# A hybrid gMLP and pooling layer on one core: edge rows loaded behind the first row tile, their norm chain placed behind the first copies, and their turned form given a tile of its own

## The chip, the core and the metric

The kernel runs on one core of one Trainium2 chip. The metric is the device time of one execution in microseconds (us). The inputs are full size: one prompt stream of 4096 frames with 1024 channels, and one sample stream of 32 frames.

## What is computed

One layer of a streaming encoder, once for the prompt and once for the sample rows:

```python
h = rmsnorm(x, norm_g)
u, v, z_a, xb, z_b = split(h @ w_in)                      # w_in: 1024 x 5120
v_n = layernorm(v, ln_v_g, ln_v_b)
a = u * chunk_mlp(v_n, w_spatial, b_spatial) * silu(z_a)  # 128x128 mixing matrix per head
x_ext = concatenate([pool_past, xb])                      # 15 earlier rows, then the new ones
b = pool_mix(x_ext, pos0, w_pool, pool_scale) * silu(z_b) # trailing means of 2/4/8/16 rows, then w_pool
y = rmsnorm(x + concatenate([a, b]) @ w_out, final_g)
```

Further outputs are the last 15 rows of `x_ext` of both streams (the pooling state) and the sample's `v_n`.

## The kernel before

**The work as a whole.** Nearly all the time goes into large matrix products in float32 accuracy. Each operand is split into a rounded part and a rest (L109 casts on ScalarE, L82 subtracts on VectorE), and a product of 2x2 blocks is made with seven block products instead of eight. Those matmuls stand at L184 and, for the output projection, at L703 to L705. The span before them, some 57 us, prepares what they need, and the change lies wholly there.

**The opening phase** has four strands, written in one loop over eight row tiles `i` (`for i in range(KT)`), whose parts a scheduler then puts in order on each engine. Some instructions are wrapped in `tc.keep_in_program_order`, which fixes their place among the others that are wrapped; the rest may be moved.

- *Combined weights.* The part of `w_in` that makes `xb` is multiplied by `w_pool`. `load_rows(i)` (L247) loads 128 rows of `w_in`, a row tile. `comb_rows(i)` turns it with eight transposes on PE (L418) into two PSUM tiles `tr` and copies each into a buffer `h` (L422; on VectorE for row tiles 0 and 1, on ScalarE from 2 on). `comb_times(i)` multiplies these by the pooling weights (L272, loaded into `op` at L261), ScalarE copies the sums out of PSUM (L436), and GpSimd stores them (L438). For row tile 0 the two halves are called apart: the first half, then row 1's transposes and whatever stands in `before[0]`, then the second half.
- *Edge rows.* The 32 sample rows and the last 16 prompt rows, 48 in all (`edge`, tile `et`), loaded at L264 and L265, with `norm_g` as rows at L266. `edge_stack` makes their RMS norm: a Square with a running sum on ScalarE (L337), one step (L338) and the eleven steps of `rsqrt` (L87 to L92) on VectorE, a scaling on ScalarE (L339). Then PE turns `norm_g` (L341) and the rows (L345), and VectorE writes the result, scaled, into a buffer `h` (L346). `State.times` multiplies it by pairs of row tiles (L192, for the pooling state), and a store to `stk` (L559) keeps it for the sample's later work.
- *v weights.* Four loads of two tiles (L283, L284), each split into seven pairs of operands in `slot` (L109, L82, with sums at L105). `PACE` says how many of these steps follow each row tile.
- *First token tiles.* Pairs of prompt tiles `xt` (L459), normed (Square at L305, scaling at L320 on VectorE) and turned (L466). The first product of the large kind follows at L184, with an operand whose rest is made by VectorE (L82, into `op`).

At the very start PE runs 14 transposes of the identity (`WARM`, L257), which compute nothing that is used.

**Buffers.** `h` tiles rotate over 8 buffers (`h_p`). One of them holds the turned edge rows from L346 until the store to `stk` has landed. Transposes use three PSUM tiles, sums five.

**Queues.** All loads of this phase are issued by SyncE, in the order of the program; the stores of combined weights are issued by GpSimd.

## Time and profile before

| | |
|---|---|
| median of 3 runs (lowest, highest) | 2330.75 us (2328.94, 2331.07) |
| the profiled execution, its span | 2328.7 us, 2326.9 us |
| PE busy, DVE busy, ACT busy | 99%, 76%, 38% of the span |
| granted TensorE clock, mean | 0.998 |
| PE's longest wait | 6.3 us, ended at 11.97 us |

The profile is of one execution. A row of its order of time has the start from the span's beginning, the length, the engine, the line of the kernel, the operation with the tiles it writes and reads, and in brackets how long the engine had been idle and what ended that. PE is TensorE, PEld its weight loads, DVE VectorE, ACT ScalarE, POOL GpSimd, SP SyncE; a small q marks the sequencer of an engine. A float32 matmul has two records, so four matmuls read as x8.

### The profile page before, as it was taken

The numbers are of one execution on the slowest core, as the hardware profiler recorded it, in microseconds if no ns is written. First come the engines' busy times: TensorE is split into PE (matmuls) and PEld (weight loads), VectorE is DVE, ScalarE is ACT, GpSimd is POOL, SyncE is SP. The second block draws the span as 40 slices with busy tenths as digits, with TensorE's granted clock in tenths as the row PEclk, the third lists the DMA queues.
The fourth block names the chain that finished last, engine by engine and source line by source line (L and its number), as shares of the span: only waits on it lengthen the run. The fifth ranks groups of instructions, "written<-read, shape, count | busy, mean of one in ns | idle before, by whom it ended". The sixth has DMA issues, their size and how long they took to land.

```text
span 2326.9 us, 30064 instructions
## 1 busy us (share of the span) xinstructions
PE 2310.8 (99%) x10723; PEld 1892.7 (81%) x10723; DVE 1763.3 (76%) x3172; ACT 893.9 (38%) x1560; POOL 224.9 (10%) x357
## 2 busy tenths in 40 slices
PE   8999999999999999999999999999999999999998
PEld 6888888878878888778888888888888878887887
DVE  6987777867787866887757977778876666588887
ACT  6554544334334333343434433434322222233343
POOL 1000001000121102221000210001200000000000
PEclk9999999999999999999999999999999999999999
DMA  8877777445549454657544483634595555846552
GB/s 281 324 274 281 288 243 247 147 147 181 175 136 352 144 176 133 211 201 254 180 145 158 127 311 120 201 109 154 184 351 169 177 187 183 334 164 205 177 168 91
DMA packets 318221, 470.62 MB, mean 202 GB/s; under 512 B 26068, under 2 KB 225244, under 8 KB 316280
## 3 DMA queue, kind: packets, MB, share of 16 engines
q1 hardware_dynamic: 266872, 379.64, 47.9%
q0 software_dynamic: 21936, 74.14, 8.7%
q10 hardware_dynamic: 29264, 14.94, 2.2%
q8 instruction: 84, 1.38, 0.2%
q14 instruction: 65, 0.53, 0.1%
HBM read 299.19 MB, written 169.47 MB: 201 GB/s over the span
## 4 chain that ended last, share of the span: by engine, by line
PE 95%; DVE 2%; DMA 2%; ACT 0%; issue 0%; SPq 0%; POOL 0%; DVEq 0%; ACTq 0%
PE acc L184 62%; PE acc L703 9%; PE acc L704 9%; PE acc L705 9%; PE sp L956 2%; PE acc L272 1%; PE tr L466 1%; PE acc L192 1%; DMA raw<-in_w_in_dram 1%; DVE wop L82 0%; PE more L192 0%; DMA xt<-in_x_prompt_dram 0%; DVE sum L105 0%; PE tr L418 0%; DMA v_smp<-raw 0%
## 5 line engine op out<-in xcount | busy, mean ns | idle before, releaser
L184 PE MATMUL acc<-slot,wop 128*128 128x512 f32 x5376 | 1240.7, 391 | 1.2 <-DVE wop L82 0.4
L184 PEld LDWEIGHTS acc<-slot,wop 128*128 128x128 f32 x5376 | 1003.3, 188 | 226.1 <-DVE t L156 10.3
L82 DVE TENSOR_TENSOR wop<-raw,wop 128x512 fp32r<-128x512 f32 x520 | 354.5, 686 | 49.7 <-ACT wop L109 43.8
L109 ACT CAST wop<-raw 128x512 fp32r<-128x512 f32 x360 | 221.4, 622 | 337.2 <-PE acc L184 256.5
L703 PE MATMUL acc<-slot,wop 128*128 128x512 f32 x892 | 347.9, 390 | 0.0
L705 PE MATMUL acc<-slot,wop 128*128 128x512 f32 x892 | 347.1, 389 | 0.0
L704 PE MATMUL acc<-slot,wop 128*128 128x512 f32 x892 | 347.0, 389 | 0.0
L184 PE MATMUL acc<-slot,op 128*128 128x512 f32 x1344 | 322.7, 395 | 0.0
L184 PEld LDWEIGHTS acc<-slot,op 128*128 128x128 f32 x1344 | 247.9, 188 | 51.0 <-DVE op L82 0.4
L156 DVE TENSOR_TENSOR t<-acc,t 128x512 f32<-128x512 f32 x256 | 175.7, 686 | 139.7 <-ACT t L165 102.5
L715 DVE TENSOR_TENSOR y<-acc,y 128x512 f32<-128x512 f32 x243 | 164.6, 688 | 133.5 <-PE acc L705 132.4
L703 PEld LDWEIGHTS acc<-slot,wop 128*128 128x128 f32 x892 | 167.4, 188 | 41.4 <-ACT wop L666 6.7
L666 ACT CAST wop<-raw 128x512 fp32r<-128x512 f32 x160 | 99.6, 622 | 252.6 <-PE acc L705 231.0
L705 PEld LDWEIGHTS acc<-slot,wop 128*128 128x128 f32 x892 | 167.4, 188 | 34.9
L704 PEld LDWEIGHTS acc<-slot,wop 128*128 128x128 f32 x892 | 167.4, 188 | 34.5
L82 DVE TENSOR_TENSOR wop<-sum,wop 128x512 fp32r<-128x512 f32 x208 | 142.4, 686 | 61.8 <-ACT wop L109 60.9
L964 POOL DMA_DIRECT2D abT<-t x128 | 69.3, 542 | 799.2 <-DVE t L974 547.0
L109 ACT CAST wop<-sum 128x512 fp32r<-128x512 f32 x144 | 89.2, 622 | 149.2 <-PE acc L184 98.7
L985 DVE TENSOR_TENSOR t<-t 128x527 f32<-128x527 f32 (+3 forms) x160 | 111.3, 696 | 0.4
L165 ACT COPY t<-acc 128x512 f32<-128x512 f32 x64 | 37.5, 585 | 125.6 <-PE acc L184 125.6
L666 ACT CAST wop<-sum 128x512 fp32r<-128x512 f32 x64 | 39.8, 622 | 105.4 <-PE acc L705 72.8
L958 DVE SCALAR_TENSOR_TENSOR t<-sp,lvg,bias 128x512 f32<-128x512 f32 x64 | 47.7, 746 | 41.8 <-PE sp L956 41.7
(210 smaller groups left out, 1872.2 us busy)
## 6 DMA issues: line engine op xcount, KB each, us to landing
raw<-in_w_in_dram SPq DMA_DIRECT2D x126, 512.0 KB, 5.1
xops<-op SPq DMA_DIRECT2D x100, 512.0 KB, 6.3
slot<-xops SPq DMA_DIRECT2D x44, 1024.0 KB, 9.3
abT<-t POOLq DMA_DIRECT2D x128, 256.0 KB, 3.0
raw<-abT SPq DMA_DIRECT2D x64, 512.0 KB, 4.5
wops<-wop SPq DMA_DIRECT2D x56, 512.0 KB, 3.8
slot<-wops SPq DMA_DIRECT2D x14, 2048.0 KB, 9.4
raw<-comb SPq DMA_DIRECT2D x38, 512.0 KB, 4.6
```

The lines of the kernel that those rows point to most:

```text
L82: return nc.vector.tensor_tensor(out, src, hi.bitcast(F32), ALU.subtract)
L109: pair = nc.scalar.copy(hi, src), lo_part(lo, src, hi)
L156: add = lambda o, x, y: nc.vector.tensor_tensor(o, x, y, ALU.add)
L184: mm(acc, stationary(s, k), moving(m, k), start=fresh and n == 0, stop=n == len(terms) - 1, skip_group_check=True)
L666: nc.scalar.copy(t[:, 0], src)
L703: mm(acc, x[:, 0, k, :], w[:, k, 0, c], start=fresh and k == 0, stop=False, skip_group_check=True)
L704: mm(acc, x[:, 0, k, :], w[:, k, 1, c], start=False, stop=False, skip_group_check=True)
L705: mm(acc, x[:, 1, k, :], w[:, k, 0, c], start=False, stop=k == 3, skip_group_check=True)
L715: nc.vector.tensor_tensor(y, self.acc[bank], y, ALU.add)
L958: nc.vector.scalar_tensor_tensor(t1[:, :HALF].rearrange("p (a c) -> p a c", c=P), sp, lg, bias[:, h:h + 1, :].broadcast_to([P, 4, P]), ALU ...
L964: nc.gpsimd.dma_start(abT[row, :, t0:t0 + HALF], t[:, :HALF])
L985: tt(nxt[:, lo:HALO + m], s[:, lo:HALO + m], s[:, lo - step:HALO + m - step], ALU.add)
```

## The change

There are five edits, all in the opening phase.

1. The three loads of the edge rows and of `norm_g` are issued right behind the two halves of row tile 0, ahead of the first two pooling weights; they stood behind these.
2. A Square of one column of the identity is put on ScalarE ahead of all else. It computes nothing that is used; the load of the activation table now belongs to it.
3. `edge_stack` is cut in two. `edge_norm` has the norm; its first VectorE step and the scaling on ScalarE are pinned, and it is called ahead of the first half of row tile 0's product. `edge_turn` has the transposes and is called behind the second half; the transposes' first, the copy of `norm_g` and the last step are pinned.
4. The turned edge rows get a tile `whole` of their own, and `h` has 7 rotating buffers instead of 8.
5. The first transpose of row tiles 2 and 3 is pinned as that of row tile 1 was.

```diff
-        h_p = ph.enter_context(tc.tile_pool(name="h_p", bufs=8))
+        h_p = ph.enter_context(tc.tile_pool(name="h_p", bufs=7))
...
         edge, g_rows = etile(), half()
+        whole = h_p.tile([P, KT * m_edge], F32, tag="stk", name="whole", bufs=1)

         load_rows(0, 2)
+        nc.sync.dma_start(edge[:DEC], xs)
+        nc.sync.dma_start(edge[DEC:m_edge], xp[SEQ - HALO:SEQ, :])
+        nc.sync.dma_start(g_rows[:KT, :P], norm_g[0].rearrange("(k p) -> k p", p=P))
+        tc.keep_in_program_order(nc.scalar.activation(small("ss", 1, P), ident[:, :1], AF.Square))
         warm = tr_tile()
...
             if q == 0:
-                nc.sync.dma_start(edge[:DEC], xs)
-                nc.sync.dma_start(edge[DEC:m_edge], xp[SEQ - HALO:SEQ, :])
-                nc.sync.dma_start(g_rows[:KT, :P], norm_g[0].rearrange("(k p) -> k p", p=P))
                 load_rows(1)
...
-        def edge_stack():
-            rows, by_g = edge[:m_edge], cols[:, 2 * KT:3 * KT]
+        def edge_norm():
+            rows = edge[:m_edge]
             ss, a = small("ss", 1, m_edge), small("na", 1, m_edge)
             junk = h_p.tile([P, D], BF16, tag="junk", name="junk", bufs=1)
             nc.scalar.activation(junk[:m_edge], rows, AF.Square, accum_out=ss)
-            nc.vector.tensor_scalar(a, ss, 1.0 / D, EPS, ALU.mult, ALU.add)
-            nc.scalar.activation(rows, rows, AF.Copy, scale=rsqrt(a, 1, m_edge))
-            tr, whole = tr_tile(), half()[:, :KT * m_edge]
-            nc.tensor.transpose(tr[:, :KT], g_rows[:KT, :P], ident[:KT, :KT])
-            nc.vector.tensor_copy(by_g, tr[:, :KT])
+            tc.keep_in_program_order(nc.vector.tensor_scalar(a, ss, 1.0 / D, EPS, ALU.mult, ALU.add))
+            tc.keep_in_program_order(nc.scalar.activation(rows, rows, AF.Copy, scale=rsqrt(a, 1, m_edge)))
+
+        def edge_turn():
+            by_g = cols[:, 2 * KT:3 * KT]
+            tr = tr_tile()
+            tc.keep_in_program_order(nc.tensor.transpose(tr[:, :KT], g_rows[:KT, :P], ident[:KT, :KT]))
+            tc.keep_in_program_order(nc.vector.tensor_copy(by_g, tr[:, :KT]))
             tr = tr_tile()[:, :KT * m_edge].rearrange("p (k m) -> p k m", k=KT)
             for k in range(KT):
                 nc.tensor.transpose(tr[:, k, :], edge[:m_edge, k * P:(k + 1) * P], ident[:m_edge, :m_edge])
...
-            stacked.append(whole)
+            by_g = by_g.rearrange("p (k t) -> p k t", t=1).broadcast_to([P, KT, m_edge])
+            tc.keep_in_program_order(
+                nc.vector.tensor_tensor(whole.rearrange("p (k m) -> p k m", m=m_edge), tr, by_g, ALU.mult))
...
-                    if i == 1 and c == 0:
+                    if i in (1, 2, 3) and c == 0:
                         tc.keep_in_program_order(turn)
...
-        before = {0: [edge_stack, lambda: load_rows(3), lambda: load_v_weights(1)],
+        before = {0: [lambda: load_rows(3), lambda: load_v_weights(1)],
...
             if i == 0:
+                edge_norm()
                 comb_times(i, parts, (0,))
             nxt = comb_rows(i + 1) if i + 1 < KT else None
             for step in before.get(i, []):
                 step()
             comb_times(i, parts, (0, 1) if i else (1,))
+            if i == 0:
+                edge_turn()
...
-        beside_pairs = {1: lambda: nc.sync.dma_start(stk, stacked[0]), 2: state.out}
+        beside_pairs = {1: lambda: nc.sync.dma_start(stk, whole), 2: state.out}
```

What the edits make of the order on the engines is seen at two places. The first is the beginning of VectorE's program, before; `h<-tr` is a copy of the turned row tile 0, and the other rows are the edge rows' norm.

```order
L338 TENSOR_SCALAR na<-ss 48x1
L87 TENSOR_SCALAR rs_t<-na 48x1
L88 TENSOR_SCALAR rs_y<-rs_t 48x1
L90 TENSOR_TENSOR rs_t<-rs_y 48x1
L422 COPY h<-tr 128x512 x2
```

And the same place in the changed kernel, where L425 is the copy that was L422.

```order
L425 COPY h<-tr 128x512 x2
L338 TENSOR_SCALAR na<-ss 48x1
L87 TENSOR_SCALAR rs_t<-na 48x1
L88 TENSOR_SCALAR rs_y<-rs_t 48x1
L90 TENSOR_TENSOR rs_t<-rs_y 48x1
```

The two copies of row tile 0 have moved from behind the first four steps of the norm to the head of VectorE's program; what follows is the same in both, down to the copies of row tile 1.

The second place is the beginning of PE's program, before: the warm-up, row tile 0's transposes, the first half of its product (L272), row tile 1's transposes, the edge rows' transposes (L341, L345) within the second half of the product, row tile 2's transposes, and the first product for the state (L192).

```order
L257 MATMUL tr<-ident 128x128 x14
L418 MATMUL tr<-ident,vt 128x128 x8
L272 MATMUL acc<-op,h 128x256 x4
L418 MATMUL tr<-ident,vt 128x128 x8
L341 MATMUL tr<-ident,h 128x8
L272 MATMUL acc<-op,h 128x256
L345 MATMUL tr<-ident,et 128x48 x8
L272 MATMUL acc<-op,h 128x256 x3
L418 MATMUL tr<-ident,vt 128x128 x8
L192 MATMUL acc<-vt,h 32x512 x4
```

In the changed kernel L262, L421, L274, L344 and L348 are the lines that were L257, L418, L272, L341 and L345.

```order
L262 MATMUL tr<-ident 128x128 x14
L421 MATMUL tr<-ident,vt 128x128 x8
L274 MATMUL acc<-op,h 128x256 x4
L421 MATMUL tr<-ident,vt 128x128 x8
L274 MATMUL acc<-op,h 128x256 x4
L344 MATMUL tr<-ident,h 128x8
L348 MATMUL tr<-ident,et 128x48 x8
L421 MATMUL tr<-ident,vt 128x128 x8
L192 MATMUL acc<-vt,whole 32x512 x4
```

The edge rows' transposes now stand behind the whole second half of row tile 0's product. Nothing else changes its place on PE. On ScalarE the first copy of sums (L436) now stands ahead of the scaling of the edge rows (L339), and in the first 57 us a few casts of v weights change places with copies of sums; the same holds for their counterparts on VectorE, among them one cast of the last v weights that now stands behind the first operand's rest instead of ahead of it. Behind this phase the order on all engines is as it was.

## The prediction

> **What bounds the kernel now.** I read the page first, then the waits of PE, then the order of time of the first 60 us. The page says that PE is the kernel:

> ```profile
> span 2326.9 us, 30064 instructions
> PE 2310.8 (99%) x10723; PEld 1892.7 (81%) x10723; DVE 1763.3 (76%) x3172; ACT 893.9 (38%) x1560; POOL 224.9 (10%) x357
> ```

> Only 16.1 us of the span have no matmul in flight, so a change that leaves the matmuls alone can win little. The list of PE's waits says where; its first row has the total, the count and the longest, in us.

> ```profile
> PE acc L272 <- DVE h L422: 6.3, 1, 6.3
> ```

> One wait of 6.3 us, ahead of the first matmuls proper (L272), is the largest piece. The order of time there (start, length, engine, line) tells its cause.

> ```profile
> 1.36 3.25 PE L257 MATMUL tr<-ident 128*128 128x128 f32 x14 [1.36 <-POOL ident masks.py:199]
> 4.40 1.26 PE L418 MATMUL tr<-ident,vt 128*128 128x128 f32 x8
> 8.15 1.28 ACT L337 ACT_TABLE_LOAD   x1 [8.15 <-DMA et<-in_x_prompt_dram]
> 10.62 0.14 DVE L338 TENSOR_SCALAR na<-ss 48x1 f32<-48x1 f32 x1 [10.62 <-ACT junk L337]
> 11.24 1.27 DVE L422 COPY h<-tr 128x512 f32<-128x512 f32 x2
> 11.97 3.52 PE L272 MATMUL acc<-op,h 128*128 128x256 f32 x8 [6.31 <-DVE h L422]
> 13.73 0.15 DVE L92 SCALAR_TENSOR_TENSOR rs_y<-rs_t,rs_y 48x1 f32<-48x1 f32 x1
> 13.97 1.15 ACT L339 ACTIVATE et<-et,rs_y 48x1024 f32<-48x1024 f32 x1 [3.38 <-DVE rs_y L92]
> 15.32 1.04 PE L418 MATMUL tr<-ident,vt 128*128 128x128 f32 x8
> 17.08 0.69 PE L345 MATMUL tr<-ident,et 48*128 48x48 f32 x8
> 20.07 1.07 PE L192 MATMUL acc<-vt,h 128*32 128x512 f32 x8
> 21.06 3.72 PE L272 MATMUL acc<-op,h 128*128 128x256 f32 x16
> ```

> Row tile 0 is turned by 5.66 (4.40+1.26), but VectorE copies it only at 11.24: the copies stand behind the first four steps of the edge rows' norm, and those wait for a table load and a Square that wait for the edge rows, landed at 8.15. PE pays a second time, in clock, as a table over windows of 3.41 us shows (window, length, busy time of PE, PEld, DVE, ACT, POOL, then granted clock, DMA share, GB/s):

> ```profile
> 4.87:8.28 3.41, 0.79 (x7) 0.55 (x5) 0.00 (x0) 0.13 (x1) 0.00 (x0) 1.00 1.01 287
> 8.28:11.69 3.41, 0.00 (x0) 0.00 (x0) 0.97 (x5) 2.30 (x3) 0.00 (x0) 0.50 1.04 357
> 11.69:15.11 3.42, 3.14 (x8) 2.53 (x8) 1.95 (x10) 1.14 (x1) 0.00 (x0) 0.50 1.13 345
> ```

> The clock was 0.50 over two whole windows, and 3.14 us of work at half speed is 1.57 us lost. So the opening holds at most 6.3 + 1.6 = 7.9 us.

> **The change part by part.** *Copies first, table load first.* The copies can start when the transposes end: 5.7 to 7.0 (1.27 us). PE then waits for the pooling weights and the row tiles, so their landings set its start. Issue rows with the time of their landing rows, from the order of time of SyncE and the DMA issues, in the order of issue: pooling weights 0 and 1, sample rows (issue alone), row tile 1, row tile 2.

> ```profile
> 1.66 0.94 SPq L261 DMA_DIRECT2D op<-in_w_pool_dram  x2
> op<-in_w_pool_dram SPq DMA_DIRECT2D x1, 256.0 KB, 4.6
> op<-in_w_pool_dram SPq DMA_DIRECT2D x1, 256.0 KB, 5.1
> 2.65 0.47 SPq L264 DMA_DIRECT2D et<-in_x_sample_dram  x1
> 4.03 0.36 SPq L247 DMA_DIRECT2D vt<-in_w_in_dram  x1
> vt<-in_w_in_dram SPq DMA_DIRECT2D x1, 512.0 KB, 6.2
> 6.31 0.35 SPq L247 DMA_DIRECT2D vt<-in_w_in_dram  x1
> vt<-in_w_in_dram SPq DMA_DIRECT2D x1, 512.0 KB, 6.5
> ```

> *Three edge loads moved ahead of two pooling weights on SyncE's queue.* They take 4.03 − 2.65 = 1.38 us of issue, so pooling weight 0 is issued at 3.04 and, with its 4.6 us, lands at 7.6; weight 1 at 3.5 + 5.1 = 8.6. Row tile 1 is issued at 4.03 either way, with the same bytes before it: 10.2. Row tile 2 lands at 12.8, and pooling weights 2 and 3, queued between the two row tiles, between them. The edge rows, issued at 1.66, land at about 6 to 7.

> *PE's new start.* First half of row 0: from 7.6, four records and, from 8.6, four more; 16 records cost 3.72 us at full clock (L272 at 21.06), so eight cost 1.9, and it ends by 9.5, or by 10.2 at half clock. Row 1's transposes: 10.2 + 1.0. Second half of row 0: to 13.0 or 13.1, by when its weights are in. The two edge transposes L341 and L345 now stand behind all of it and cost 0.2 + 0.7: 13.9. Row 2's transposes: 14.9. L192 starts at 14.9 instead of 20.07: 5.1 us earlier. The edge chain covers this: Square from about 7, nine more small steps (10.62 to 13.88, less the 1.27 of copies: 2.0 us), ScalarE's copy of row 0 and L339's 1.15 are over by 11 or 12, and PE reaches L345 at 13.2. The warm-up square on ScalarE costs nothing: the engine is idle until 8.15.

> *What is late next.* From here to 57 us PE is full, and loads and casts must follow it. The same windows later:

> ```profile
> 18.50:22.50 4.00, 4.00 (x27) 2.71 (x26) 2.03 (x4) 3.11 (x6) 0.67 (x1) 1.00 0.38 135
> 22.50:51.00 28.50, 28.50 (x177) 22.40 (x176) 24.51 (x48) 24.44 (x49) 4.62 (x9) 1.00 1.01 345
> 51.00:57.00 6.00, 5.96 (x37) 5.14 (x36) 5.74 (x10) 4.92 (x10) 0.57 (x1) 1.00 0.06 19
> ```

> The DMA engines are full from 22.5 to 51 and idle for 62% of the 4 us before, so the loads of that stretch can come at most 2.5 us earlier while PE wants 5.1. The stores of combined weights, which follow PE and now come sooner, take part of that; I take 2.2, nearer the bound, since one such store is 512 KB, 1.5 us at 345 GB/s, and only a part of it falls ahead. What the last loads feed:

> ```profile
> 33.56 4.58 SPq L284 DMA_DIRECT2D op<-in_w_in_dram  x1
> DMA to landing us min/median/max: 6.8/9.1/12.0
> 46.96 2.47 DVE L320 SCALAR_TENSOR_TENSOR xt<-xt,rs_y,g_bc 128x1024 f32<-128x1024 f32 x2
> 51.49 1.04 PE L466 MATMUL tr<-ident,xt 128*128 128x128 f32 x8
> 51.16 0.69 DVE L105 TENSOR_TENSOR h<-op 128x512 f32<-128x512 f32 x1 [1.73 <-DMA stk<-h]
> 56.17 0.68 DVE L82 TENSOR_TENSOR op<-tr,op 128x512 fp32r<-128x512 f32 x1
> ```

> The last v weights (issued 33.56, 12.0 us to landing: 45.6) release a cast on ScalarE, this a step on VectorE, and behind that in VectorE's order stand the norms L320, done at 49.4. PE turns the second of these tiles in the second half of its 1.04 us from 51.49, at 51.9, or 2.4 us later. With the loads 2.2 us earlier the norms are done at 47.2, and PE's advance is capped at 2.2 + 2.4 = 4.6.

> *Own tile, `h` buffers 8 to 7.* Before, one of eight `h` buffers held the turned edge rows, and VectorE waited for the store of it to land (51.16, 1.73 us). Now it starts the last v weights behind L320. From 51.16 to 56.85 that block took 5.7; one of its nine steps now stands behind the step that frees PE's next stage (L184), −0.7. From 47.2 it ends at 52.2 against 56.85: 4.65 us earlier, about the same cap. Seven rotating buffers remain as before, so fewer cost nothing.

> *The pins on row tiles 2 and 3* leave PE's order as it was there: nothing.

> *The sum.* 5.1 gained at the opening, capped to 4.6 at 47 to 57 us. Behind that, orders are the same and loads are started by PE's own progress (DMA share 0.06 from 51 to 57), so it lasts. The profiled execution took 2328.7 (span 2326.9 plus 1.8): 2324.1. The median of the runs shown is 2.05 above it; carried whole it gives 2326.15. I can name one part that differs from run to run, where the clock's windows fall (1.57 us here), and it should shrink. I take 2325.6, nearer the first.

> [...] The windows above had the clock fall after 0.79 busy us of 3.41. [...] If the new windows fall as the old ones did, they hold 0.8 + 0.7 = 1.5 us (44%) and 1.2 + 1.5 = 2.7 us (79%); no row shows on which side 44% lies, and the sum above takes it as busy. Were it idle, the first rival holds.

> **The rivals.** *The clock falls all the same.* If it falls at 8.28, the first half still ends as row tile 1 lands, and row 1's transposes pay 0.7: gain 4.4, 2325.8, chance 0.12. If it falls at 11.69, 3.4 us run at half speed: 1.7, gain 3.4, 2326.8, chance 0.08. [...]

> *ScalarE and the DMA queue give it back later.* ScalarE's third v-weight cast (21.77) needs the load queued just ahead of the one in the first two rows; the last two rows are ScalarE's copies of row tile 4 and PE's transposes of row tile 5.

> ```profile
> 13.30 1.34 SPq L284 DMA_DIRECT2D op<-in_w_in_dram  x1
> op<-in_w_in_dram SPq DMA_DIRECT2D x2, 512.0 KB, 6.8
> 21.77 0.64 ACT L109 CAST slot<-op 128x512 fp32r<-128x512 f32 x1
> 32.90 1.07 ACT L422 COPY h<-tr 128x512 f32<-128x512 f32 x2
> 34.47 1.04 PE L418 MATMUL tr<-ident,vt 128*128 128x128 f32 x8
> ```

> That neighbour lands at 13.3 + 6.8 = 20.1, so this one, 1.5 us of transfer ahead, at about 18.6 (an estimate), which PE's advance does not move. The cast, due at 16.6 (21.77 − 5.1), waits 2 us; the first store of combined weights, now 5 us earlier, can add its 1.5 us. The copies that free PSUM for PE queue behind that cast. PE's slack over them is the 1.5 us from the first copy's end (33.4) to the second half of the transposes (34.9). So it feels between 0 and 2 us; with 2: gain 2.6, 2327.6.

> *No cap:* the queue drains faster than I think: gain 5.2, 2325.0.

> *Slower:* the same wait, longer. Each us by which that load lands past 18.1 (16.6 + 1.5) costs PE one. At 23.2 all 5.1 are gone; at 28 the kernel is 4.8 us slower than before, which is 9.4 above the forecast: 2335.0. Its load would have to be 9 us late, where the DMA share was at 1.0 already.

> **How the numbers follow.** The rivals' times are 2325.6 plus what their gain lacks of 4.6. Chances: forecast 0.50; clock falls 0.20; given back 0.17; no cap 0.10; slower 0.03. 0.2%, about what a measurement of this kernel can tell from no change, is 4.66 us: below 2326.1 lie 0.7 of the forecast, 0.4 of the clock cases, nearly all without a cap, little else: 0.53. Slower by over 4.66 us takes the last rival: 0.03. The rest is 0.44. The range reaches from the uncapped 5.1 with none of the median's excess (2323.6) to the case given back with all of it (2328.15), and 0.2 on each side for the spread: 2323.4 to 2328.3.

> **What would show it.** PE's wait at L274 ends by 7.5 to 9 on a DMA of `op`, not on VectorE; PEclk 1.00 from 8.28 to 18.5; L192 at 14.9; the last v weights land near 43; VectorE has no wait for `stk`; L184 starts at 52.3. Wrong: L192 after 16.5, PE gaps between 20 and 50 us, or L184 after 54.

## The result and the profile after

The changed kernel takes 2321.97 us (median of 6 runs, 2321.54 to 2322.73); beside it the kernel before took 2330.11 (6 runs, 2328.94 to 2331.07). The ratio is 0.9965, 95% interval 0.9953 to 0.9978: 8.1 us less, and 3.6 below the forecast, outside its range. The profiled execution of the changed kernel took 2321.93 (span 2320.1), 6.8 less than that of before. The median of before lies 1.4 above its profiled execution; that of the changed kernel does not.

The list of PE's waits of the changed kernel (total, count, longest):

```profile
PE tr L421 <- DMA vt<-in_w_in_dram: 1.9, 1, 1.9
PE tr L262 <- POOL ident masks.py:199: 1.4, 1, 1.4
PE acc L184 <- DVE wop L82: 0.4, 1, 0.4
PE acc L274 <- DMA op<-in_w_pool_dram: 0.3, 1, 0.3
```

The 6.3 us on VectorE is gone; what is left in the opening is a wait for row tile 1 and a short one for a pooling weight. The order of time of the same kernel shows the chain that was turned round, and further on the places where the forecast expected trouble.

```profile
5.50 1.30 DVE L425 COPY h<-tr 128x512 f32<-128x512 f32 x2 [5.50 <-PE tr L421]
5.66 1.06 ACT L337 ACTIVATE junk<-et 48x1024 bf16<-48x1024 f32 x1 [3.42 <-DMA et<-in_x_prompt_dram]
6.35 1.97 PE L274 MATMUL acc<-op,h 128*128 128x256 f32 x8 [0.28 <-DMA op<-in_w_pool_dram]
9.11 1.15 ACT L339 ACTIVATE et<-et,rs_y 48x1024 f32<-48x1024 f32 x1 [0.17 <-DVE rs_y L92]
10.26 1.06 PE L421 MATMUL tr<-ident,vt 128*128 128x128 f32 x8 [1.94 <-DMA vt<-in_w_in_dram]
13.13 0.69 PE L348 MATMUL tr<-ident,et 48*128 48x48 f32 x8
14.78 1.06 PE L192 MATMUL acc<-vt,whole 128*32 128x512 f32 x8
...
19.04 0.62 ACT L109 CAST slot<-op 128x512 fp32r<-128x512 f32 x1 [2.67 <-DMA op<-in_w_in_dram]
29.85 0.42 PEld L421 LDWEIGHTS tr<-ident,vt 128*128 128x128 f32 x4 [0.31 <-ACT h L425]
43.41 2.47 DVE L322 SCALAR_TENSOR_TENSOR xt<-xt,rs_y,g_bc 128x1024 f32<-128x1024 f32 x2
51.62 6.59 PE L184 MATMUL acc<-slot,op 128*128 128x512 f32 x26
```

L192 starts at 14.78 and was at 20.07: 5.3 earlier. L184 starts at 51.62 and was at 56.87: the 5.3 is still there. Windows of this kernel (window, length, busy time of PE, PEld, DVE, ACT, POOL, then granted clock, DMA share, GB/s):

```profile
5.69:9.10 3.41, 2.35 (x11) 1.58 (x10) 2.91 (x14) 1.71 (x3) 0.00 (x0) 1.00 0.81 235
9.10:12.52 3.42, 2.27 (x15) 2.14 (x16) 1.29 (x2) 1.15 (x1) 0.00 (x0) 1.00 1.04 367
...
17.10:22.50 5.40, 5.40 (x34) 3.93 (x33) 3.62 (x7) 3.46 (x7) 0.00 (x0) 1.00 1.03 366
22.50:47.50 25.00, 24.93 (x157) 19.91 (x156) 22.48 (x46) 22.27 (x46) 4.63 (x9) 1.00 1.02 359
47.50:51.00 3.50, 3.50 (x19) 3.04 (x18) 3.38 (x6) 3.45 (x8) 0.57 (x1) 1.00 0.03 11
```

The clock stays at 1.00 over two windows with PE busy 69% and 66%. The DMA engines have no idle stretch near 20 us any more, and are done at 47.5, where they were busy until 51.

With the PE instructions of both traces laid side by side, the lead of the changed kernel is 5.43 us from 68.6 us on. It grows by 0.61 at 582 and 0.71 at 946 and then stays. The two steps are waits which before has and the changed kernel has not, in this list of PE's waits, before:

```profile
PE acc L184 <- ACT t L163: 0.4, 1, 0.4
PE acc L184 <- DVE t L156: 0.3, 1, 0.3
```

Each is behind a cast (L109) on ScalarE that waited for the store of a split weight to land, 1.67 us at 578.20 and 4.06 at 945.50; the lead grows there by somewhat more than the waits that the list has. So three parts were to be explained: the opening (5.4), these waits (1.3), and the difference between profiles and medians (1.4).

### The profile page after: what moved, and what is told of

Its sections match the earlier page's. It is cut to its first block, busy times and chain, and to the rows that moved or that the text cites. A ratio compares the mean times of both kernels' runs of the same rounds, so it can differ in the third digit from the quotient of the medians.

```text
span 2320.1 us, 30063 instructions
## 1 busy us (share of the span) xinstructions
PE 2309.0 (100%) x10723; PEld 1892.3 (82%) x10723; DVE 1765.5 (76%) x3172; ACT 896.5 (39%) x1561; POOL 227.0 (10%) x357
## 3 DMA queue, kind: packets, MB, share of 16 engines
q8 instruction: 84, 1.38, 0.2%
## 4 chain that ended last, share of the span: by engine, by line
PE 97%; DMA 1%; DVE 1%; SPq 0%; ACT 0%; issue 0%; DVEq 0%; ACTq 0%
PE acc L184 66%; PE acc L709 9%; PE acc L711 9%; PE acc L710 9%; PE sp L962 2%; PE tr L469 1%; DMA op<-in_w_in_dram 1%; PE acc L192 1%; PE more L192 0%; DMA vt<-in_w_in_dram 0%; DVE wop L82 0%; DVE xt L322 0%; DVE slot L82 0%; SPq L247 0%; PE tr L421 0%
## 5 line engine op out<-in xcount | busy, mean ns | idle before, releaser
L184 PE MATMUL acc<-slot,wop 128*128 128x512 f32 x5376 | 1240.1, 391 | 0.4 <-DVE wop L82 0.4
L184 PEld LDWEIGHTS acc<-slot,wop 128*128 128x128 f32 x5376 | 1003.6, 188 | 224.5 <-DVE t L156 9.6
L82 DVE TENSOR_TENSOR wop<-raw,wop 128x512 fp32r<-128x512 f32 x520 | 355.3, 688 | 50.7 <-ACT wop L109 43.3
L109 ACT CAST wop<-raw 128x512 fp32r<-128x512 f32 x360 | 222.0, 623 | 337.7 <-PE acc L184 256.3
L184 PE MATMUL acc<-slot,op 128*128 128x512 f32 x1344 | 322.8, 395 | 0.1
L184 PEld LDWEIGHTS acc<-slot,op 128*128 128x128 f32 x1344 | 247.8, 188 | 51.3 <-DVE op L82 0.5
L82 DVE TENSOR_TENSOR wop<-sum,wop 128x512 fp32r<-128x512 f32 x208 | 142.8, 688 | 61.4 <-ACT wop L109 60.3
L109 ACT CAST wop<-sum 128x512 fp32r<-128x512 f32 x144 | 89.4, 624 | 145.5 <-PE acc L184 99.3
## 6 DMA issues: line engine op xcount, KB each, us to landing
raw<-in_w_in_dram SPq DMA_DIRECT2D x126, 512.0 KB, 4.9
xops<-op SPq DMA_DIRECT2D x100, 512.0 KB, 6.3
abT<-t POOLq DMA_DIRECT2D x128, 256.0 KB, 3.0
raw<-abT SPq DMA_DIRECT2D x64, 512.0 KB, 4.5
wops<-wop SPq DMA_DIRECT2D x56, 512.0 KB, 3.8
raw<-comb SPq DMA_DIRECT2D x38, 512.0 KB, 4.5
```

The costliest lines, as they stand in the source:

```text
L82: return nc.vector.tensor_tensor(out, src, hi.bitcast(F32), ALU.subtract)
L109: pair = nc.scalar.copy(hi, src), lo_part(lo, src, hi)
L184: mm(acc, stationary(s, k), moving(m, k), start=fresh and n == 0, stop=n == len(terms) - 1, skip_group_check=True)
```

## The experiments

**Before, once more.** No edit.

> The kernel before once more, unchanged, for a second profile and its own spread. What is open: the two profiled runs differ by 6.8 us, of which 5.4 arise in the opening and 1.3 at two waits of PE near 582 and 946 us; the medians differ by 8.1, because the median of before is 1.4 above its profiled run and that of after is not above its own. Theory 1, the clock's phase: the first products at 11.97 ran 3.14 us at half clock here because a window boundary stood at 15.11; the boundary stands elsewhere in other runs, so the half-clock stretch behind 11.97 varies between almost 0 and about 6.5 us, the loss between 0 and 3.3 us, and the times of before spread over about 2 us. This profile then shows another length of that stretch, and the span differs from 2326.9 by half the difference of the lengths. Theory 2, chance in the stores: the waits at 582 and 946 come and go from run to run; they are absent here, or stand elsewhere, and the span is up to 1.3 us shorter for it. Rival to both: boundary and waits are where they were, the span is 2326.9 within 0.3, and the first profile was no special run.

Median 2329.86 (11 runs, 2327.55 to 2332.24; ratio to before, 33 runs at 2329.59, 1.0002, 0.9994 to 1.0011). The profiled execution had a span of 2328.5, 1.6 more than the first. Its windows and two of its PE waits:

```profile
9.53:12.95 3.42, 1.12 (x3) 0.94 (x4) 2.26 (x10) 0.92 (x2) 0.00 (x0) 0.50 1.09 368
12.95:16.36 3.41, 3.41 (x12) 2.77 (x11) 0.65 (x5) 1.73 (x2) 0.00 (x0) 0.50 1.10 374
```

```profile
PE acc L184 <- DVE t L156: 1.3, 1, 1.3
PE acc L184 <- ACT t L163: 0.8, 1, 0.8
```

The same opening now ran 1.12 + 3.41 = 4.53 us of work at half clock, where the first profile had 3.14: 0.7 more lost. The two later waits are 2.1 in place of 0.8: 1.3 more. The half-clock stretch does lie elsewhere in this run, from 9.53 on instead of 8.28, as Theory 1 says. But its 0.7 does not last: with both traces laid side by side, this run is 0.55 us behind the first at L192 (20.62), 0.30 at the first L184 (57.17), and level with it from 69 us on, where the first waited 0.28 for a norm. The whole difference of 1.6 arises later, 1.2 between 570 and 584 and 0.4 near 946, as Theory 2 says.

**Copies first alone**, on the kernel before; L338 is pinned too, so that it cannot pass the copies.

```diff
-            nc.vector.tensor_scalar(a, ss, 1.0 / D, EPS, ALU.mult, ALU.add)
+            tc.keep_in_program_order(nc.vector.tensor_scalar(a, ss, 1.0 / D, EPS, ALU.mult, ALU.add))
...
-                (nc.scalar.copy if i > 1 else nc.vector.tensor_copy)(cols[q], tr)
+                copied = (nc.scalar.copy if i > 1 else nc.vector.tensor_copy)(cols[q], tr)
+                if i == 0:
+                    tc.keep_in_program_order(copied)
```

> The kernel before, with one part of the change alone: the copies of row tile 0 ahead of the edge rows' norm on VectorE (all four copies of row tiles 0 and 1 come to stand ahead). Loads, table load, the shared buffer and its wait stay. Theory that the copies' place is the whole gain: PE starts its products at about 6.4 as in the changed kernel (weights landed at 6.2), the clock never falls, the time is 2322 to 2323. By the prediction's own account the edge chain (table load at 8.15, Square, then VectorE's steps behind copies of row tile 1, done near 12.5 to 14) then meets PE at the edge transposes, near 13, and costs up to 1 to 2 us, and the wait for the shared buffer keeps the block at 51 to 57 us late, a further 0.7: 2323.5 to 2325. Rival, the parts are needed together: the edge chain holds PE at the edge transposes for the 3 us that table load and Square take, 2326 or more.

Median 2329.41 (ratio 1.0001, 0.9992 to 1.0010): nothing gained. Its order of time and windows show where the gain went:

```profile
7.05 1.97 PE L272 MATMUL acc<-op,h 128*128 128x256 f32 x8 [1.41 <-DMA op<-in_w_pool_dram]
13.75 1.14 ACT L109 CAST slot<-op 128x512 fp32r<-128x512 f32 x2 [0.30 <-DMA op<-in_w_in_dram]
14.80 1.14 ACT L339 ACTIVATE et<-et,rs_y 48x1024 f32<-48x1024 f32 x1
15.99 1.09 PE L345 MATMUL tr<-ident,et 48*128 48x48 f32 x8 [3.16 <-ACT et L339]
```

```profile
11.61:15.03 3.42, 1.22 (x6) 0.74 (x4) 1.88 (x15) 1.86 (x4) 0.67 (x1) 1.00 1.13 364
15.03:18.44 3.41, 2.45 (x15) 2.36 (x16) 1.90 (x4) 1.32 (x2) 0.00 (x0) 0.50 1.05 336
18.44:21.86 3.42, 3.42 (x14) 1.25 (x13) 3.42 (x6) 1.79 (x4) 0.00 (x0) 0.50 1.10 360
```

PE starts 4.9 us earlier, and then stands at the edge transposes for 3.16. That leaves a window 36% busy, the clock falls behind it, and 2.45 + 3.42 us of work run at half speed, 2.9 lost. The rival held, with the clock on top, which no theory had there. But not all of the 3.16 is table load and Square: the norm's last step ends at 13.72, and ScalarE runs two casts of v weights ahead of the scaling L339, which costs 1.1. On VectorE the norm's first step stands behind the copies of row tile 1 and starts at 11.56, 0.75 after the Square's sum. In the changed kernel the norm is called earlier, and both of these steps are pinned.

**The wait filled**, on the kernel before.

```diff
         parts = comb_rows(0)
+        fill = acc_tile()
+        for _ in range(52):
+            tc.keep_in_program_order(nc.tensor.transpose(fill[:, :P], ident, ident))
...
-                    if i == 1 and c == 0:
+                    if i < 2 and c == 0:
```

> The kernel before, with 52 more transposes of the identity on PE in the wait ahead of its first products; they fill 5.7 to about 12.3 and write a tile that is not read. PE starts as late as before, only the clock should stay up. Theory 1 (clock's phase): the granted clock is 1.00 from 5 us to the end; against the profiled run of before 1.6 us are saved, less about 0.5 if the fill overruns 11.97, and against its median 1.6 to 3: 2327 to 2328.5, with a spread under 1.2 us. Rival, the clock's loss is not what lies between before's median and its profile: the gain against the median is 1.6 or less, 2328.5 to 2329. Second rival, the clock does not count these transposes: it falls as before and the time is 2330. The order of some loads and of casts on ScalarE after 13 us is changed by the scheduler as a side effect; if PE shows new waits between 13 and 60 us, the run says less.

Median 2327.42 (2326.16 to 2329.62), ratio 0.9990 (0.9982 to 0.9999): 2.2 us less than before, by the interval 0.2 to 4.2. PE starts L272 at 12.03 instead of 11.97, and the clock is 1.00 in the windows that hold the fill:

```profile
5.18:8.59 3.41, 3.41 (x33) 3.41 (x32) 0.00 (x0) 0.38 (x1) 0.00 (x0) 1.00 0.95 283
8.59:12.00 3.41, 2.91 (x27) 2.67 (x25) 1.22 (x6) 2.05 (x3) 0.00 (x0) 1.00 0.98 325
```

So holding the clock is worth about 2.2 on the median, with that wide interval. In the profiles it is 1.3: that much is PE ahead of the first profile of before from 69 us on. That profile had lost 1.57 to the clock, the least of the three profiles of this opening (the third is below).

**The changed kernel, started late.**

```diff
-WARM = 14
+WARM = 64
```

> The changed kernel, with a longer warm-up on PE: 64 transposes of the identity instead of 14. PE turns row tile 0 some 6.4 us later (50 x 0.127), while loads and the other engines go on as they do; clock held. If what the opening gains stays to the end, and the loads set no bound, this loses what PE starts later by less the 1.94 us that PE now waits for row tile 1 and 0.28 for a weight: 6.4 - 2.2 = about 4.2, 2326 to 2326.5. If loads between 20 and 57 us bound the kernel (the prediction's cap), part of the later start costs nothing: below 2325.5. Theory 2' (the waits near 582 and 946 belong to a late opening rather than to chance): they come back here and the time is 1.3 higher, 2327.3 to 2328; by Theory 2 they are absent or elsewhere.

Median 2327.07 (2325.98 to 2328.15), 5.1 above the changed kernel, more than expected. L274 starts 5.56 later (11.91), L192 3.5 later (18.24), and then a row tile comes late for PE by 0.97 at 29.45, and a wait of 0.5 stands near 582. The late row tile is not the start's doing alone: the scheduler issued the third pair of v weights (14.56, 17.09) ahead of it (21.19). With both traces laid side by side, PE is 4.1 us later than in the changed kernel from 60 us on, and 5.3 later from 1307 us on. So with the clock held throughout, a late opening costs 5.1 on the median, of which some 4.1 arise in the opening. Start and clock, 5.1 and 2.2, are together 7.3 of the 7.6 between 2329.59 and 2321.97.

**The edge edits undone, one by one**, on the changed kernel. First the three edge loads, put back behind the first two pooling weights:

```diff
-        nc.sync.dma_start(edge[:DEC], xs)
-        nc.sync.dma_start(edge[DEC:m_edge], xp[SEQ - HALO:SEQ, :])
-        nc.sync.dma_start(g_rows[:KT, :P], norm_g[0].rearrange("(k p) -> k p", p=P))
...
             if q == 0:
+                nc.sync.dma_start(edge[:DEC], xs)
+                nc.sync.dma_start(edge[DEC:m_edge], xp[SEQ - HALO:SEQ, :])
+                nc.sync.dma_start(g_rows[:KT, :P], norm_g[0].rearrange("(k p) -> k p", p=P))
```

> The changed kernel with the three edge loads back behind the first two pooling weights; table load, order and tile as changed. With the copies first alone on the kernel before, the edge rows landed at 8.36 and PE waited 3.16 us for the scaled edge rows, behind a table load of 1.28, a Square of 1.06 and 12 steps of VectorE; the clock then fell and everything was given back. Here the table load is out of that chain: Square from about 8.2 to 9.5, VectorE's twelve steps to 11.7, L339 to 12.9, PE reaches L348 at 13.13. Theory A (each of the edge edits takes about 1.3 to 3 us out of one chain, and the chain needs only the first microsecond of it): no cost, 2322.0 within 0.4. Theory B (the early loads are what lets PE go on): the chain ends past 13.1 and costs PE 1 us or more, 2323 or more. The pooling weights should land no earlier than the 6.22 they have in the changed kernel, where edge loads stand ahead of them; if they land earlier by the 1.38 us of issue that the prediction charged, PE starts no earlier all the same, as it has the copies at 6.1.

Median 2321.72 (2320.73 to 2322.87; ratio to before 0.9968): no cost. Pooling weight 0 landed at 6.39, behind no edge load; with the three loads ahead of it, it landed at 6.22. What the early loads do move is row tile 1: without them in front, PE's wait for it is 0.59 instead of 1.94. PE then waits 0.43 for L339, still comes to the large products 0.8 us earlier than in the changed kernel, and loses 0.9 of its lead near 940, around a wait of 0.62. So the early loads are no gain by themselves in these runs. Then the small Square taken out:

```diff
-        tc.keep_in_program_order(nc.scalar.activation(small("ss", 1, P), ident[:, :1], AF.Square))
```

> The changed kernel without the small first Square on ScalarE, so that the table load waits for the edge rows again (landed 5.57): Square at 6.9 instead of 5.66, VectorE's steps end at 10.3, L339 at 11.5, PE reaches the edge transposes at 13.13. Theory A: hidden, 2322.0 within 0.4. Theory B (each part is needed): 1.3 us lost, 2323.3.

Median 2322.55 (2322.15 to 2323.03), 0.6 above the changed kernel, a little outside what was expected; PE's waits differ by 0.3 at 54.6 us, not at the edge transposes. Then both edits undone together:

> The changed kernel with both undone: edge loads behind the two pooling weights, and no first Square, so the chain is table load from about 8.2, Square, 12 steps to about 12.9, L339 to 14.2; copies first, PE order and own tile as changed. Theory A: now the chain is longer than its cover and PE waits at L348 from 13.13 to 14.2: 1.1 us, 2323.1 (2322.8 to 2323.6). [...] Theory B': copies first alone failed for another reason than this chain (the scheduler's other moves there): no cost, 2322.0.

Median 2324.02 (2322.86 to 2325.74), 2.1 above. PE waits for L339, here L338, and the clock falls behind a window that is 60% busy:

```profile
12.76 1.15 ACT L338 ACTIVATE et<-et,rs_y 48x1024 f32<-48x1024 f32 x1 [1.69 <-DVE rs_y L92]
13.96 0.69 PE L347 MATMUL tr<-ident,et 48*128 48x48 f32 x8 [1.35 <-ACT et L338]
```

```profile
11.95:15.36 3.41, 2.06 (x19) 1.58 (x18) 2.55 (x9) 2.60 (x5) 0.67 (x1) 1.00 1.12 374
15.36:18.78 3.42, 3.42 (x14) 1.26 (x13) 3.38 (x6) 1.94 (x5) 0.00 (x0) 0.50 1.09 338
```

Theory A's wait is there, 1.35 us where it gave 1.1; the clock fell besides, to 0.50 from 15.36 to 18.78, which loses half of that, 1.7 us, and the time lies 0.4 above Theory A's range. Either edit is enough. And with neither, the kernel is still 4.8 us faster than before beside it (2328.83): what the copies first alone had not must do that, the pinned places of the norm and of the transposes and the own tile; the runs part off only the tile, below.

**The own tile undone**: the turned edge rows in one of eight `h` buffers.

```diff
-        h_p = ph.enter_context(tc.tile_pool(name="h_p", bufs=7))
+        h_p = ph.enter_context(tc.tile_pool(name="h_p", bufs=8))
...
-        whole = h_p.tile([P, KT * m_edge], F32, tag="stk", name="whole", bufs=1)
+        stacked = []
...
         def edge_turn():
             by_g = cols[:, 2 * KT:3 * KT]
+            whole = half()[:, :KT * m_edge]
+            stacked.append(whole)
```

> The changed kernel with the turned edge rows in one of eight rotating half tiles again. VectorE then waits for the store of them (landed 47.99 in the changed kernel) before a step of the last v weights. By the prediction's account the block at the first operands ends 0.7 to 1.7 us later and PE, which had no slack there, loses as much: 2322.7 to 2323.7. Rival: PE had 0.1 us of wait on VectorE at 55 us and the rest is slack, so nothing is lost: 2322.0 within 0.4. Both: if the waits near 582 and 946 us (0.3 to 1.5 us in three profiles of late openings, none in the changed kernel) are chance, some of these four kernels show them; if they belong to an opening that is late by 4 us or more, none does.

Median 2323.45 (2322.06 to 2325.72), 1.5 above. In the order of time VectorE waits for the store of the edge rows again, and PE stands behind it, two stages on:

```profile
48.03 0.69 DVE L105 TENSOR_TENSOR h<-op 128x512 f32<-128x512 f32 x1 [2.20 <-DMA stk<-h]
53.34 0.66 PE L471 MATMUL tr<-ident,xt 128*128 128x128 f32 x4 [2.03 <-ACT h L496]
```

```profile
6.97:10.38 3.41, 1.80 (x10) 1.30 (x9) 1.79 (x13) 1.73 (x2) 0.00 (x0) 1.00 0.90 280
51.34:54.76 3.42, 1.42 (x8) 1.25 (x9) 3.33 (x6) 2.92 (x6) 0.77 (x2) 1.00 0.31 129
54.76:58.17 3.41, 3.41 (x9) 2.64 (x8) 3.33 (x6) 2.63 (x5) 0.34 (x1) 0.50 1.01 284
```

The profiled execution is the longest of the eleven (2325.72): it lost 2.03 us to this wait, and half of the window of 3.41 behind it. On the median the tile is worth 1.5, within the 0.7 to 1.7 that was expected.

**The changed kernel, once more.** No edit.

> The changed kernel once more, unchanged. The waits near 582 and 946 us: 0.78, 2.10 and 1.59 us in three profiles of kernels whose opening fell to half clock, 0.66 in one that starts as late without the fall, and 0, 0.62, 0, 0.52 and 0.42 in five of early openings. Chance (theory 2): this profile shows 0 to 0.7, and times from 2321 to 2323. The opening is the same in every run but for the landing of row tile 1 (9.1 to 10.3 in the profiles): L192 at 14.0 to 14.9, clock 1.00 throughout, since the windows with PE busy 53% and more held it in all profiles and those with 42% and less did not.

Median 2321.88 (5 runs, 2321.62 to 2322.65); no wait near 582 or 946, clock 1.00, L192 at 14.54. That 53% and more held the clock in all profiles is not so: with both edge edits undone it fell behind a window 60% busy.

**A ninth buffer for split weights**, on both kernels, paid for in two other pools.

```diff
-    op_p = pool("wop_p", 8)
+    op_p = pool("wop_p", 9)
...
-        t_p = pool("t_p", 10, ph)
+        t_p = pool("t_p", 9, ph)
...
-        y_p = pool("y_p", 6, ph)
+        y_p = pool("y_p", 5, ph)
```

> The kernel before with nine buffers instead of eight for the split output weights (paid for with one of ten temporaries of the spatial stage and one of six output tiles), so that ScalarE's casts at 555 to 980 us wait less for the stores of those tiles. Theory 2: the two waits of PE near 582 and 946 us are these stores' and go; 0.8 to 2.1 us less, 2327.5 to 2328.8 with a narrower spread, if the two smaller pools cost nothing. Rival: the waits are late loads of raw weights, which a buffer more does not bring earlier: both waits stay and the time is 2329.5. Against both, the fewer temporaries or output tiles cost something after 1600 us.

> The same edit on the changed kernel. Theory 2: it had none of these waits in its profile and at most 0.6 in three of its near relatives, so 0 to 0.4 is gained: 2321.5 to 2322. If the difference of before_wop9 to this one is 5.4 + 0.8 (the opening as profiled and the mean of the half-clock stretch over its length here), about 6.2, the three parts (opening, clock, store waits) make up the whole 7 to 8 us between the medians; if it stays at 7.5 or more, the waits are not a part.

On before 2329.52 (ratio 0.9997, 0.9989 to 1.0006), on the changed kernel 2323.65, 1.7 more than without. The wait near 582 is still there on before, with 1.43; the one near 946 is gone, and the smaller pools cost PE 0.2 there and 0.7 on the changed kernel, at 2060 us. The changed kernel also has 1.1 of new waits near 956 and 1285 us, whose cause is not shown. The experiment did not settle these waits, and its sum of parts can't be drawn. What it did show, in the windows of before with nine buffers, is a third amount of work at half clock:

```profile
11.03:14.44 3.41, 2.23 (x5) 1.83 (x6) 2.77 (x13) 0.22 (x1) 0.00 (x0) 0.50 1.12 354
14.44:17.85 3.41, 3.41 (x14) 2.59 (x12) 0.80 (x2) 1.51 (x2) 0.00 (x0) 0.50 1.10 364
```

2.23 + 3.41 = 5.64 us at half clock: 2.8 lost, after 1.6 and 2.3 in the two profiles of before.

**Edge loads on ScalarE's queue**, on the changed kernel; in a second run with the other loads up to 45 us, and the store to `stk`, pinned in the changed kernel's order.

```diff
-        nc.sync.dma_start(edge[:DEC], xs)
-        nc.sync.dma_start(edge[DEC:m_edge], xp[SEQ - HALO:SEQ, :])
-        nc.sync.dma_start(g_rows[:KT, :P], norm_g[0].rearrange("(k p) -> k p", p=P))
+        nc.scalar.dma_start(edge[:DEC], xs)
+        nc.scalar.dma_start(edge[DEC:m_edge], xp[SEQ - HALO:SEQ, :])
+        nc.scalar.dma_start(g_rows[:KT, :P], norm_g[0].rearrange("(k p) -> k p", p=P))
```

> The changed kernel with its three edge loads issued by ScalarE's queue, which stands idle, so SyncE issues pooling weights and row tile 1 at once (row tile 1 at about 2.7 instead of 3.94). What is left of PE's waits in the opening of the changed kernel is 1.94 for row tile 1 and 0.28 for a weight. If issue is what holds row tile 1: it lands up to 1.3 us earlier and 1 us is gained, 2321. If the transfers hold it (DMA share 0.92 and more from 2.3 us): 0 to 0.4, 2321.6 to 2322. Side effect: the scheduler moves a few casts of v weights and steps of a norm on VectorE and ScalarE between 20 and 57 us, which can cost 0 to 1 us at the first operands; then 2322.5.

Median 2326.92 (2324.78 to 2328.42), 5 us above the changed kernel, missed by everything expected. Row tile 1 did land at 8.39 instead of 10.12. But the scheduler put the third pair of v weights ahead of row tile 4 on SyncE's queue. Rows of PE, and the window in which they stand:

```profile
25.02 0.63 PE L421 MATMUL tr<-ident,vt 128*128 128x128 f32 x4 [1.74 <-DMA vt<-in_w_in_dram]
26.94 1.11 PE L421 MATMUL tr<-ident,vt 128*128 128x128 f32 x4 [1.29 <-ACT h L425]
```

```profile
22.80:26.21 3.41, 1.11 (x7) 0.50 (x5) 2.30 (x4) 3.41 (x8) 0.02 (x1) 1.00 1.03 399
```

The pins of the second run, on these loads and in the same way on those of row tiles, `norm_g`, the state and the first two pairs of prompt tiles:

```diff
-            nc.sync.dma_start(a, w_in_v[:, :, c0:c0 + P])
+            tc.keep_in_program_order(nc.sync.dma_start(a, w_in_v[:, :, c0:c0 + P]))
```

> Edge loads on ScalarE's queue, and the order of the other loads up to 45 us held as in the changed kernel, so that row tile 4 is not pushed behind the third pair of v weights (there it landed at 24.89 and PE waited 1.74 and 1.29, with the clock at half for 6.8 us behind). PE's waits in the opening were 1.81 there against 3.08 and 3.58 in the changed kernel. If no cap holds PE between 20 and 57 us: 1.3 to 1.7 us gained, 2320.3 to 2320.7. If the loads that are full from 22 us on hold it (the prediction's cap, one us further on): waits of PE at 24 to 55 us take it back, 2321.5 to 2322.

With the order held, 2322.17 (2322.12 to 2323.96): no better than the changed kernel. The profiled execution is 1.15 above this median (2323.32). In it PE is 1.4 us ahead of the changed kernel at the first L184 and still 0.9 at the 400th, so most of the earlier start is kept; later it loses more, at 577 and 941 us:

```profile
PE acc L184 <- DVE t L156: 1.3, 1, 1.3
PE acc L184 <- ACT t L163: 0.3, 1, 0.3
```

**Later still**, the changed kernel.

```diff
-WARM = 14
+WARM = 76
```

> The changed kernel with 76 warm-up transposes: twelve more than with 64 (x 0.127), PE starts 1.5 us later than there, and as late as the kernel before is after its half-clock stretch. By the start alone: 2327.07 + 1.5 = 2328.6, waits near 582 and 946 at 0 to 0.8. If these waits go with a late opening: 0.8 to 2.1, and 2329 to 2330.

Median 2333.33, profiled execution 2330.04: slower than both expectations, and than before (ratio 1.0013, 1.0004 to 1.0022). There is no wait near 582 or 946. What it has is this, in its order of time:

```profile
21.09 0.62 ACT L109 CAST slot<-op 128x512 fp32r<-128x512 f32 x1 [3.26 <-DMA op<-in_w_in_dram]
21.74 0.69 DVE L82 TENSOR_TENSOR slot<-op,slot 128x512 fp32r<-128x512 f32 x1 [3.96 <-ACT slot L109]
22.35 0.16 DVE L345 COPY cols<-tr 128x8 f32<-128x8 f32 x1
22.56 0.65 PE L421 MATMUL tr<-ident,vt 128*128 128x128 f32 x4 [2.65 <-DVE cols L345]
```

The scheduler here let a rest (L82) pass the small copy L345, and the rest waits for a cast that waits for a v-weight load, issued at 14.14 as the third of its kind. PE loses 2.65 us to it. The prediction's *slower* rival feared such a load, but another one, on another path: the second of its kind, by way of ScalarE's copies. In the changed kernel that one came at 19.01, with 2.67 of wait on ScalarE, and no such loss on PE. Why the other ten runs are 3 us longer than the profiled one, no profile shows.

**The wait filled with small transposes**: as the fill above, with 72 transposes of 48 columns.

```diff
+        for _ in range(72):
+            tc.keep_in_program_order(nc.tensor.transpose(fill[:, :48], ident[:48, :], ident[:48, :48]))
```

> The kernel before with the wait ahead of its products filled with 72 transposes of 48 columns (0.086 each, 6.2 us) in place of the 52 of 128 columns. If every transpose counts as busy for the clock, as 128 columns did: 1.00 from 5 us on, 2327.4. If transposes of 48 columns count little: the clock falls behind the first window of them, the transposes and the products after them run at half speed, PE starts its products 3 us later, 2330 to 2333. The order of some loads and casts behind 20 us differs between the two by the scheduler's choice, so the clock in the profile tells more than the time.

Median 2328.90 (ratio 0.9994, 0.9985 to 1.0003), between the two; the profiled execution is the shortest of the eleven (2327.36). The clock in its windows:

```profile
7.49:10.90 3.41, 2.40 (x39) 2.27 (x37) 0.67 (x5) 2.43 (x3) 0.00 (x0) 1.00 0.99 342
10.90:14.31 3.41, 2.84 (x7) 2.27 (x8) 2.24 (x10) 0.83 (x1) 0.00 (x0) 0.50 1.14 365
```

Behind a window 70% busy with nothing but 48-column transposes the clock fell to 0.50; in one 53% busy, mostly with products, it was 1.00 (the window from 6.97 under the own tile), and that run's mean granted clock was 0.999.

## Why the prediction was wrong

Its sum was 2328.7 − 4.6 + 1.5 = 2325.6. What happened is 2328.7 − 5.43 − 1.32 = 2321.95. Three terms failed, 0.8 + 1.3 + 1.5 = 3.6: the cap on the opening's gain, the "so it lasts" that put everything behind the opening at nothing, and the 1.5 carried for the median. The range had room for the first and the last, since its lower end has neither a cap nor any of the median's excess. It had none for the 1.3 behind the opening, and that is nearly all of what lies below it.

- **The opening was right.** L192 was given 14.9 and came at 14.78, row tile 1 at 10.2 and 10.12, the edge transposes at 13.2 and 13.13, the clock stayed up. One landing was wrong: pooling weight 0 at 7.6, because 1.38 us of issue were charged to it. It landed at 6.22; the late loads show that it would have landed no earlier without the edge loads in front. PE's order of work was not changed by it, but that the clock held may be: with 7.6, the prediction counted a window 44% busy and took that as enough, and later runs fell behind 42% and held behind 53%. The windows that came were 69% and 66% busy. In this the forecast had some luck.
- **The cap failed as a size.** The step that failed here reads "I take 2.2": the loads of 22 to 51 us came earlier by more. The last norms start at 43.41 instead of 46.96, 3.55 earlier, where the prediction has 2.2. The stretch of 4 us that was 62% idle gave its 2.5, as counted; the rest came from the transfers themselves, 359 GB/s from 22.5 to 47.5 where there were 345, on 28.5 us some 1.1. With 2.4 of slack behind the loads the cap is 5.95, above the 5.3 that PE wanted. The *no cap* rival had the mechanism right; its time, 2325.0, missed by the other two terms.
- **The own tile was needed**: 1.5 us on the median. The 0.7 beside it in the prediction is for a step of VectorE's that changes place, and came out: that block took 5.08 (45.80 to 50.88) instead of 5.7.
- **ScalarE's wait was there and did no harm.** Predicted: load at 18.6, 2 us. Measured: 19.01, 2.67 us. From 22.5 to 47.5 PE was idle 0.07 in all, at 29.85.
- **The median's excess was carried the wrong way.** The prediction named the place of the clock's windows as the part that differs from run to run, said that it should shrink, and still carried 1.5 of 2.05. Over the six runs of before the excess is 1.4, over the changed kernel's it is 0. That this place varies is shown: in three profiles of the opening before the clock fell at 8.28, 9.53 and 7.61, and half clock cost them 1.6, 2.3 and 2.8. That this makes the excess is not. Of the 0.7 that the second lost more than the first nothing was left at 69 us, of the third's 1.2 there was 0.85, and the rest of their excess came from later waits. Filling the wait won 2.2 on the median, but anything from 0.2 to 4.2 fits that. What the excess is made of stays open.
- **"Behind that, orders are the same … so it lasts"** held for the 5.43, but 1.3 came on top from the two later waits, which before has and the changed kernel has not. In kernels built on before they are 0.8 and 2.1 us in its two profiles, 1.4 with nine buffers, 1.6 with the copies first alone, and 0 and 1.0 under the two fills. In those built on the changed kernel they are 0 in both of its profiles, without the Square, with nine buffers and in the later start; 0.4 to 0.6 in the late start, with the late loads, with both edge edits undone, without the own tile and with the edge loads on ScalarE's queue; and 1.65 with those loads pinned. Neither a late opening nor an early one is what makes them, and a ninth buffer did not take the first away. What sets them stays open. As near relatives of the changed kernel show 0.4 to 0.6, some of the 1.3 may be luck of the profiled executions; that is not shown.

## What to carry to other kernels

When one chain is moved out of another's way, cost it together with the chain that then comes late: the copies alone won nothing, 4.8 us came with the chain's steps pinned and its tile apart, and with either of two edits on the chain nearly everything. Where the clock has fallen, one profile shows one place of the fall (8.28, 9.53 and 7.61 in three of them), and what it loses there has to be followed further: 0.7 us more lost at 13 us was gone at 69. A scheduler's order of loads is part of an edit: a longer warm-up and another queue for three small loads cost PE waits of 2.65 and 3.0 us here, each by an instruction that passed another.

## What the runs showed of the hardware

A window is here a stretch of 3.41 us of a trace. In the windows shown, the stretches at half clock have this length or two or three times as much: 3.42 us with both edge edits undone (15.36 to 18.78), 6.83 in the first profile of before (8.28 to 15.11) and with the copies first (15.03 to 21.86), 10.24 in before with nine buffers (7.61 to 17.85). What half clock costs is seen at the first eight records of L272: 3.52 us in before, of which 3.14 lay at 0.50, and 1.97 at 1.00 in the changed kernel.

Two windows do not fit the order of the shares, 60% (both edge edits undone) and 70% (the small fill): in the one 0.85 of the 2.06 us, in the other all, were transposes with 48 columns or fewer. Transposes of 128 columns did hold the clock: over two windows of nothing else, 100% and 85% busy, the fill has it at 1.00, with a mean of 0.999 over the run. The small ones have 48 rows as well as 48 columns, so which of the two matters is not told apart.

Once down, the clock stayed down behind windows 65% (before with nine buffers), 72% (copies first) and 79% busy (edge loads on ScalarE's queue), and it was 1.00 again behind one 92% busy (before, from 15.11 on).
